# A two-layer hybrid transformer on one core: an out-projection put in program order, and two operations of the attention moved

## The chip, the cores and the metric

The kernel runs on one core of a Trainium2 chip. The metric is the device time of one execution in microseconds (us), given as the median of several runs. One further execution was taken by the hardware profiler; every row below comes from it, with times counted from the start of its span. The engines are TensorE (PE in the profile; its weight loads are PEld), VectorE (DVE), ScalarE (ACT), GpSimd (POOL) and SyncE (SP), which here issues most DMAs.

## The reference, cut to what matters

Layer 0 is grouped-query attention over 512 latent and 256 context tokens, followed by a gated FFN; layer 1 is a bidirectional Mamba-2 SSD mixer, followed by a gated FFN. The change touches the attention's inner loop and the SSD's last step.

```python
def gqa_attend(q, k, v):
    s = jnp.einsum('bqhgd,bkhd->bhgqk', q, k).astype(jnp.float32) * (HEAD_DIM ** -0.5)
    p = jax.nn.softmax(s, axis=-1).astype(v.dtype)
    return jnp.einsum('bhgqk,bkhd->bqhgd', p, v)
...
        y = yf + flip(yb) + d_skip[..., None] * xs
        y = rms_norm(y.reshape(bsz, length, D_INNER) * jax.nn.silu(z), norm_w) @ w_out
```

The out-projection takes 2048 gated values per token (D_INNER) to 1024 (D_MODEL); RMSNorm stands ahead of it. The model has 16 query heads of 64 and 4 key-value heads.

## The kernel before

Activations lie transposed, features on the 128 partitions and tokens along the free axis (L = 512 latent, C = 256 context, T = 768 together). A product of a weight tile and an activation tile is made of three matmuls, so that its precision is near float32: both operands are split into a high part (wh, and for activations names such as yh, hhy, qh) and a low part (wl, yl, hly, ql). `split` (L82 to L88) makes them: ScalarE casts the high part (L85), VectorE or GpSimd subtracts it from the original for the low part (L87). `load_w` loads a weight tile of 128 x 1024 (wst) and splits it; wst, wh and wl share one rotation of 10 buffers. `mm3` (L103) then issues wh times the high part (L108), wh times the low part (L109) and wl times the high part (L111).

The program is written as Python generators that are advanced by turns, and a scheduler then sets each engine's order from data dependencies and the order of the program; so an instruction can stand elsewhere than it is written. `behind(g, a, b)` adds a dependency of order alone: a comes after b on its engine.

**Attention.** The 16 heads are worked in 8 pairs p. `Pair.maxima` computes the scores once for their row maxima (ps_m, L643; VectorE's reduction ma and mb, L645) and puts the negated maxima on a diagonal (diag, L666). `Pair.steps` computes for each of 7 steps the scores of a key block for both heads (ps_s, L715) and adds the diagonal (L717); ScalarE takes the exponential of 128 x 1024 (pr, L718); VectorE adds it to a running sum (acc, L723 and L725); TensorE multiplies by the values (ps_o, L679). At a pair's end the sums come from a matmul (ps_sum, L685), ScalarE makes their reciprocal by logarithm and exponential (y, L688 and L689), and VectorE scales and corrects the output (o and u, L690 to L692). The scores have two PSUM buffers, shared by ps_s and ps_m: a score group waits for the exponential or the reduction that empties its buffer. The list `exps` holds the exponentials issued so far. Queries of later pairs are prepared beside this: `queries(p)` normalises and rotates the queries of pair p and splits them (qs to qh and ql, 128 x 768). For p from 4 to 7 the queries are also projected late: `qproj(p)` loads a weight tile, splits it with GpSimd making the low part, and projects (ps_q). The first of these, p = 4, is cast at a place in the values loop ahead of the pairs (`i == 30`).

**SSD's out-projection.** It stands at the end of `ssd` (L1290 on). Its 16 activation tiles are the gated products z times a norm weight, split by `ysplit` (ScalarE L1300, VectorE L1301) into hhy0 to hhy7 with their low parts hly, and, for the last eight, yh and yl. Their squares (ysq, L1231) are summed by GpSimd, and their row sums by TensorE (ssy, L247) give the norm's factor rsy, applied to the output. The loop over kp = 0 to 7 loads one weight tile each (wout0), covers two activation tiles k and four output tiles (`pm`, in ps_wo_13890 and ps_wo_13891): 2 x 4 x 3 = 24 matmuls. At kp == 4 output tile m = 4 is begun: `wm(4)` loads two weight tiles more (their high parts are wh_14141 and wh_14147), and `m_tile` runs its k = 0 to 7, again 24 matmuls, with hhy0 to hhy7 into ps_wo_14152. Its k = 8 to 15 follow behind the row sums, then the tiles m = 5 to 7. The weights of kp == 4 are wh_14135 and wl_14136.

Of the kernel before, what the change touches and what calls it, by code (L numbers as in the profile page):

```python
# [7 lines left out]
P = 128  # L8
# [7 lines left out]
D = 1024  # L16
KT = D // P
L = 512
# [62 lines left out]
def split(g, src, hi, lo, lo_engine="dve", pin=False):  # L81

    nc = g.nc
    keep = g.tc.keep_in_program_order if pin else lambda i: i
    cast = keep(nc.scalar.copy(hi, src))  # L85
    eng = nc.vector if lo_engine == "dve" else nc.gpsimd
    keep(eng.tensor_tensor(lo, src, _r(hi), ALU.subtract))  # L87
    return cast  # L88
# [14 lines left out]
def mm3(g, w, outs, first, last):  # L103

    wh, wl = w
    mm = g.nc.tensor.matmul
    for out, (ah, al) in outs:
        mm(out, wh, ah, start=first, stop=False)  # L108
        mm(out, wh, al, start=False, stop=False)  # L109
    for out, (ah, al) in outs:  # L110
        mm(out, wl, ah, start=False, stop=last)  # L111


def ada(g, src, layer, chunks, m0, nm, big=True):
# [111 lines left out]
def behind(g, bi, other):  # L226
    g.tc.add_manual_dep(bi.ins, other.ins.name, mybir.DependencyInfo(
        mybir.DependencyClass.NoSync, mybir.DependencyReason.DATA), reason="kept behind")
# [3 lines left out]
    follow(g, g.nc.scalar.preload_act_table_set("natural_log_exp_and_others"))  # L232


def rstd_rows(g, sq, n, cols, width, name, bank):

    nc = g.nc
    c = cols.shape[-1]  # L240
    nt = n // P
    ps = bank(f"ss{name}")
    w = nt * c
    sq = sq if isinstance(sq, list) else [sq]
    for i, part in enumerate(sq):
        for t in range(nt):
            nc.tensor.matmul(ps[:, i * w + t * c : i * w + (t + 1) * c], part[:, t * P : (t + 1) * P], cols,  # L247
                             start=True, stop=True)
    small = lambda nm: g.p.tile([P, nt * c], F32, tag="rst", bufs=8, name=nm)
    a, y, u = small("rsa"), small("rsy"), small("rsu")  # L250
    nc.vector.tensor_scalar(a, ps[:, :w], 1.0 / width, EPS, ALU.mult, ALU.add)
    if len(sq) == 2:
        nc.vector.scalar_tensor_tensor(a, ps[:, w : 2 * w], 1.0 / width, a, ALU.mult, ALU.add)

    for f in ((lambda: nc.scalar.activation(y, a, AF.Ln)), (lambda: nc.scalar.activation(y, y, AF.Exp, scale=-0.5))):
        g.root = f()
        if g.tables:
            follow(g, g.root)
    nc.vector.tensor_tensor(u, y, a, ALU.mult)
    nc.vector.scalar_tensor_tensor(u, y, -0.5, u, ALU.mult, ALU.mult)  # L260
    if c == 1:
        nc.vector.scalar_tensor_tensor(a, u, 1.5, y, ALU.add, ALU.mult)
        root = lambda t: a[:, t : t + 1].broadcast_to([P, P])
    else:
        rb = t3(g, f"rb{name}", n=n)
        wide = lambda v: v.unsqueeze(2).broadcast_to([P, nt * c, P // c])
        nc.vector.scalar_tensor_tensor(rb.rearrange("p (a b) -> p a b", b=P // c), wide(u), 1.5, wide(y),
                                       ALU.add, ALU.mult)
        root = lambda t: rb[:, t * P : (t + 1) * P]
    yield BREAK  # L270
    for t0 in range(0, nt, 4):
        pt = bank(f"rsT{name}")
        for t in range(t0, min(nt, t0 + 4)):
            nc.tensor.transpose(pt[:, (t - t0) * P : (t - t0 + 1) * P], root(t), g.ident)
        yield (pt, t0 * P, min(n, (t0 + 4) * P))
# [52 lines left out]
def Bank(g, name):  # L328
    return g.ps.tile([P, 512], F32, tag="B", bufs=4, name=name)
# [71 lines left out]
def attention(g, fill, X, late):  # L401


    nc, I = g.nc, g.I
# [61 lines left out]
    for m in range(KT):  # L466
        sq = t2("sql") if m else sums[0]
# [5 lines left out]
    norm = rstd_rows(g, sums, L, g.ones[:, :1], D, "a", Bk)  # L473
# [25 lines left out]
    for m in range(KT):  # L499
# [5 lines left out]
        if m in (1, 2):  # L505
            for a in range(4 * m - 4, 4 * m):
                sq = t2("sqc")[:, :C] if a else sqc
# [3 lines left out]
        if m == 3:  # L511
            norm = rstd_rows(g, sqc, C, g.ones[:, :1], D, "a", Bk)
# [73 lines left out]
    qprep = {}  # L586
# [3 lines left out]
    exps = []  # L590

    def qproj(p):

        st = t4(g, "wst")
        nc.sync.dma_start(st, I["wq"][p - 4])
        yield
        w = t4(g, "wh", F32R), t4(g, "wl", F32R)
        cast = split(g, st, *w, lo_engine="pool")
        if exps:
            behind(g, cast, exps[-1])  # L600
        yield
        qs = t3(g, "qs")
        for h, c0, n in ((hc, L, C), (hl, 0, L)):
            ps = Bk("ps_q")
            for k in range(KT):
                ks = slice(k * P, (k + 1) * P)
                mm3(g, (w[0][:, ks], w[1][:, ks]), [(ps[:, :n], h[k])], k == 0, k == KT - 1)
                yield 3 * n / 2400
            nc.scalar.copy(qs[:, c0 : c0 + n], ps[:, :n])
        qraw[p] = qs  # L610

    def queries(p, eng):
        qs = qraw[p]
        yield from normed(qs, g.qn8, eng)
        qprep[p] = t3(g, "qh", F32R), t3(g, "ql", F32R)
        split(g, qs, *qprep[p])
        yield 0

    onesr = g.const.tile([P, P], F32R, name="onesr")
# [116 lines left out]
    for n, j in enumerate((0, 1, 2, 4, 5, 3)):  # L736
        ps = Bk("ps_c")
# [73 lines left out]
    m = pairs[0].maxima()  # L811
    for i, _ in enumerate(vals):
        if i % 5 == 2:
            next(m, None)
        if i % 6 == 5:
            next(qgen[1], None)
        if i in (12, 26, 30, 34):
            next(qgen[2], None)
        if i == 16:
            next(side)  # L820
        if i == 30:
            next(items[1])
    for gen in (m, qgen[1], qgen[2]):
        for _ in gen:
# [2 lines left out]
    for p in range(NH // 2):  # L827
        m = iter(())
        if p < 7:
            m = pairs[p + 1].maxima()  # L830
# [165 lines left out]
def ssd(g, x, norm, wf, bg, close):  # L996


    nc, I, tc = g.nc, g.I, g.tc
# [4 lines left out]
    pool = lambda n, **k: ph.enter_context(tc.tile_pool(name=n, bufs=1, **k))  # L1004
# [20 lines left out]
    ps = ps_dt  # L1025
# [27 lines left out]
    for i in range(0, P, H2):  # L1053
        f, b = slice(i, i + 32), slice(i + 32, i + 64)
# [59 lines left out]
    acc = [None]  # L1114
# [125 lines left out]
    for gi in range(8):  # L1240
        i = -1
# [52 lines left out]
    ys = []  # L1294
# [17 lines left out]

    po = [S(g, "ps_wo") for _ in range(2)]
    pm = [po[i // 2][:, (i % 2) * 512 : (i % 2) * 512 + L] for i in range(4)]
    def m_tile(m, ws, ps, a, b, ks, bg=iter(())):
        for k in ks:
            c0 = (k % 8) * P
            mm3(g, tuple(w[:, c0 : c0 + P] for w in ws[k // 8]), [(ps, tuple(t[:, a:b] for t in ys[k]))],
                k == 0, k == 15)
            if k % 2:  # L1320
                next(bg, None)

    wm = lambda m: [load_w(g, I["wout1"][m - 4, i]) for i in range(2)]
    for kp in range(8):
        w = load_w(g, I["wout0"][kp])
        if kp == 4:
            ws, ps = wm(4), Bank(g, "ps_wo")
            m_tile(4, ws, ps, 0, L, range(2 * 4))
        for kk in range(2):
            ysplit()  # L1330
            k = 2 * kp + kk
            for i in range(4):
                c0 = kk * 512 + i * P
                mm3(g, (w[0][:, c0 : c0 + P], w[1][:, c0 : c0 + P]), [(pm[i], ys[k])], k == 0, k == 15)
        next(prev, None)
    ln_exp(g)
    norm = rstd_rows(g, acc[0], L, g.ones[:, :1], 2 * D, "y", lambda nm: Bank(g, nm))
    next(norm)
    m_tile(4, ws, ps, 0, L, range(2 * 4, 16))
    nc.scalar.copy(rs, next(norm)[0])  # L1340
# [6 lines left out]
    for m in (4, 5):  # L1347
        if m > 4:
            ws, ps = wm(m), Bank(g, "ps_wo")
# [7 lines left out]
    for seg in SEGS[0]:  # L1357
        _, a, b = seg
# [199 lines left out]
```

## Time and profile before

| What | us |
|---|---|
| runs of the kernel | 1860.58, 1860.64, 1859.17 |
| their median | 1860.58 |
| the profiled execution | 1859.79 |
| its span in the profile | 1858.0 |

In rows of the timeline the columns are the start, the duration, the engine, the line, the operation, output <- inputs, the shapes, and the count of merged instructions; brackets hold the idle time of the engine just before and what ended it. Times are in us from the span's start. Matmul rows of one group overlap, since a matmul starts before the one ahead of it has drained.

### The profile page before, as it was taken

What the parts mean: (1) busy time and instruction counts of PE and PEld (TensorE: products, weight loads), DVE (VectorE), ACT (ScalarE), POOL (GpSimd) and SP (SyncE); (2) the same over time, 40 slices, a digit from 0 to 9 for tenths busy, and PEclk for the clock granted to TensorE, in tenths of its full rate; (3) what the DMA queues carried; (4) which work ended last, traced back from release to release, by engine and by line L of the source; (5) the groups of instructions that cost most, each with busy time, mean ns of one, the idle gap of its engine ahead of it and who ended that gap; (6) DMA issues with size and microseconds to landing.
All of it is one profiled execution on the core that took longest, in us unless ns stands there. A gap on an engine that the chain in (4) does not pass through costs nothing.

```text
span 1858.0 us, 28773 instructions
## 1 busy us (share of the span) xinstructions
PE 1837.9 (99%) x11454; PEld 1540.3 (83%) x11454; DVE 1302.8 (70%) x1978; ACT 809.9 (44%) x1424; POOL 286.6 (15%) x260
## 2 busy tenths in 40 slices
PE   9999999999999999999999999999999999999999
PEld 7975656798888888888998888888887888888887
DVE  5578888788777776455487787777797566565655
ACT  4544434363222222222367666776666352323231
POOL 0223110030000000000133333444433100000000
PEclk9999999999999999999999999999999999999999
DMA  9323241124434553121224433444362223232232
GB/s 348 91 96 111 63 170 52 58 92 170 141 131 153 188 182 113 57 68 50 65 83 140 136 109 88 123 125 124 103 181 92 79 91 114 91 100 95 90 105 89
DMA packets 74071, 211.68 MB, mean 114 GB/s; under 512 B 9040, under 2 KB 14544, under 8 KB 73808
## 3 DMA queue, kind: packets, MB, share of 16 engines
q1 hardware_dynamic: 73936, 209.84, 35.0%
q8 instruction: 90, 1.47, 0.3%
q14 instruction: 45, 0.37, 0.1%
HBM read 198.79 MB, written 6.82 MB: 111 GB/s over the span
## 4 chain that ended last, share of the span: by engine, by line
PE 87%; DVE 6%; DMA 3%; issue 2%; ACT 1%; POOL 1%; SPq 0%; DVEq 0%; POOLq 0%; ACTq 0%
PE ps_up L108 10%; PE ps_up L111 10%; PE ps_up L109 10%; PE ps_d L108 7%; PE ps_d L109 6%; PE ps_d L111 6%; PE ps_in L111 5%; PE ps_in L109 5%; PE ps_in L108 4%; PE ps_s L715 2%; PE ps_o L679 2%; PE ps_st L1150 2%; PE ps_wo L109 1%; PE ps_wo L108 1%; PE ps_wo L111 1%
## 5 line engine op out<-in xcount | busy, mean ns | idle before, releaser
L87 DVE TENSOR_TENSOR wl<-wst,wh 128x1024 fp32r<-128x1024 f32 x207 | 258.5, 1249 | 202.8 <-PE ps_up L109 105.3
L85 ACT CAST wh<-wst 128x1024 fp32r<-128x1024 f32 x211 | 221.0, 1048 | 333.8 <-DMA wst<-in_wup 263.4
L108 PE MATMUL ps_up<-hhf,wh 128*128 128x512 f32 x1008 | 355.9, 353 | 0.0
L109 PE MATMUL ps_up<-hlf,wh 128*128 128x512 f32 x1008 | 355.8, 353 | 0.0
L111 PE MATMUL ps_up<-hhf,wl 128*128 128x512 f32 x1008 | 355.8, 353 | 0.0
L111 PEld LDWEIGHTS ps_up<-hhf,wl 128*128 128x128 f32 x1008 | 190.7, 189 | 25.9
L108 PEld LDWEIGHTS ps_up<-hhf,wh 128*128 128x128 f32 x1008 | 189.2, 188 | 25.9
L109 PEld LDWEIGHTS ps_up<-hlf,wh 128*128 128x128 f32 x1008 | 189.2, 188 | 25.9
L108 PE MATMUL ps_in<-hhs,wh 128*128 128x512 f32 (+1 forms) x560 | 203.7, 364 | 1.0 <-ACT dt L1035 1.0
L109 PE MATMUL ps_in<-hls,wh 128*128 128x512 f32 (+1 forms) x560 | 198.6, 355 | 0.0
L111 PE MATMUL ps_in<-hhs,wl 128*128 128x512 f32 (+1 forms) x560 | 198.3, 354 | 0.0
L108 PE MATMUL ps_d<-hdh,wh 128*128 128x512 f32 (+1 forms) x568 | 193.2, 342 | 0.8 <-DVE X L892 0.5
L109 PE MATMUL ps_d<-hdl,wh 128*128 128x512 f32 (+1 forms) x568 | 193.4, 341 | 0.0
L111 PE MATMUL ps_d<-hdh,wl 128*128 128x512 f32 (+1 forms) x568 | 192.8, 340 | 0.0
L892 DVE SCALAR_TENSOR_TENSOR X<-ps_d,mod,X 128x512 f32<-128x512 f32 (+1 forms) x224 | 125.2, 587 | 35.0 <-PE ps_d L111 34.3
L108 PEld LDWEIGHTS ps_in<-hhs,wh 128*128 128x128 f32 x560 | 105.5, 188 | 16.0 <-ACT dt L1035 1.2
L108 PEld LDWEIGHTS ps_d<-hdh,wh 128*128 128x128 f32 x568 | 106.5, 188 | 14.0 <-DVE X L892 0.9
L109 PEld LDWEIGHTS ps_d<-hdl,wh 128*128 128x128 f32 x568 | 106.9, 188 | 13.2 <-DVE hdl L87 0.4
L111 PEld LDWEIGHTS ps_d<-hdh,wl 128*128 128x128 f32 x568 | 107.6, 189 | 12.2
L111 PEld LDWEIGHTS ps_in<-hhs,wl 128*128 128x128 f32 x560 | 105.2, 188 | 14.8
L109 PEld LDWEIGHTS ps_in<-hls,wh 128*128 128x128 f32 x560 | 105.4, 188 | 13.4
L718 ACT ACTIVATE pr<-ps_s 128x1024 f32<-128x1024 f32 x56 | 57.2, 1022 | 105.1 <-PE ps_s L717 105.1
(343 smaller groups left out, 3629.8 us busy)
## 6 DMA issues: line engine op xcount, KB each, us to landing
wst<-in_wup SPq DMA_DIRECT2D x88, 512.0 KB, 3.4
wada<-in_adaT SPq DMA_DIRECT2D x56, 512.0 KB, 3.5
wst<-in_win SPq DMA_DIRECT2D x48, 512.0 KB, 3.6
wst<-in_wdown SPq DMA_DIRECT2D x44, 512.0 KB, 3.7
E<-ad SPq DMA_DIRECT2D x64, 256.0 KB, 6.6
wada<-in_adaB SPq DMA_DIRECT2D x24, 512.0 KB, 4.2
ec<-ead SPq DMA_DIRECT2D x64, 128.0 KB, 6.4
wst<-in_wout SPq DMA_DIRECT2D x16, 512.0 KB, 3.4
```

The lines of the kernel that those rows point to most:

```text
L85: cast = keep(nc.scalar.copy(hi, src))
L87: keep(eng.tensor_tensor(lo, src, _r(hi), ALU.subtract))
L108: mm(out, wh, ah, start=first, stop=False)
L109: mm(out, wh, al, start=False, stop=False)
L111: mm(out, wl, ah, start=False, stop=last)
L679: nc.tensor.matmul(po[S64[e], :n], v, pr[:, 512 * e + off : 512 * e + off + n], start=first, stop=last)
L715: nc.tensor.matmul(outs[e], kk[e][a][S64[e], k], b[S64[e], q], start=i == 0, stop=False)
L718: exps.append(nc.scalar.activation(pr, ps, AF.Exp))
L892: nc.vector.scalar_tensor_tensor(ap, o[:, c0:c1], gate[:, m, v : v + 1], ap, ALU.mult, ALU.add)
L1150: nc.tensor.matmul(ps[:, d * 256 : (d + 1) * 256], Bt[:, t * P : (t + 1) * P], xw[d][t], start=t == ts[0], stop=t == ts[-1])
```

## The change

There are three edits. First, `mm3` returns its matmuls, and in the out-projection `in_line` puts each group of three behind the group written before it; this covers the kp loop and output tile 4. The row sums are put behind the last group of the kp loop. Second, for p = 7 the cast of the queries is put behind the last exponential issued when it is written. Third, the low part of the first late query weights is made by VectorE, not GpSimd, and its place in the values loop moves from `i == 30` to `i == 36`.

```diff
     for out, (ah, al) in outs:
-        mm(out, wh, ah, start=first, stop=False)
-        mm(out, wh, al, start=False, stop=False)
+        seq.append(mm(out, wh, ah, start=first, stop=False))
+        seq.append(mm(out, wh, al, start=False, stop=False))
     for out, (ah, al) in outs:
-        mm(out, wl, ah, start=False, stop=last)
+        seq.append(mm(out, wl, ah, start=False, stop=last))
+    return seq
...
-            nc.tensor.matmul(ps[:, i * w + t * c : i * w + (t + 1) * c], part[:, t * P : (t + 1) * P], cols,
-                             start=True, stop=True)
+            mm = nc.tensor.matmul(ps[:, i * w + t * c : i * w + (t + 1) * c], part[:, t * P : (t + 1) * P], cols,
+                                  start=True, stop=True)
+            if after:
+                behind(g, mm, after)
...
-        cast = split(g, st, *w, lo_engine="pool")
+        cast = split(g, st, *w, lo_engine="pool" if exps else "dve")
...
-        split(g, qs, *qprep[p])
+        cast = split(g, qs, *qprep[p])
+        if p == 7:
+            behind(g, cast, exps[-1])
...
-        if i == 30:
+        if i == 36:
             next(items[1])
...
+    line = []
+
+    def in_line(seq):
+        if line:
+            behind(g, seq[0], line[-1])
+        line[:] = seq[-1:]
+
     def m_tile(m, ws, ps, a, b, ks, bg=iter(())):
         for k in ks:
             c0 = (k % 8) * P
-            mm3(g, tuple(w[:, c0 : c0 + P] for w in ws[k // 8]), [(ps, tuple(t[:, a:b] for t in ys[k]))],
+            seq = mm3(g, tuple(w[:, c0 : c0 + P] for w in ws[k // 8]), [(ps, tuple(t[:, a:b] for t in ys[k]))],
                 k == 0, k == 15)
+            if m == 4:
+                in_line(seq)
...
-                mm3(g, (w[0][:, c0 : c0 + P], w[1][:, c0 : c0 + P]), [(pm[i], ys[k])], k == 0, k == 15)
+                in_line(mm3(g, (w[0][:, c0 : c0 + P], w[1][:, c0 : c0 + P]), [(pm[i], ys[k])], k == 0, k == 15))
         next(prev, None)
     ln_exp(g)
-    norm = rstd_rows(g, acc[0], L, g.ones[:, :1], 2 * D, "y", lambda nm: Bank(g, nm))
+    norm = rstd_rows(g, acc[0], L, g.ones[:, :1], 2 * D, "y", lambda nm: Bank(g, nm), after=line[-1])
```

Line numbers of the changed kernel are higher: L108, L109 and L111 become L109, L110 and L112; L718 becomes L724, L688 L694, L1231 L1237, and L1300 L1306. Numbers behind a name tell its buffers apart.

ScalarE in the attention's last pairs but one, before: qh_3176 is the cast of the queries of p = 7, pr the exponentials, y the first step of a pair's end.

```order
L718 ACTIVATE pr_3076<-ps_s_3075 128x1024
L718 ACTIVATE pr_3137<-ps_s_3136 128x1024
L85 CAST qh_3176<-qs_2544 128x768
L718 ACTIVATE pr_3159<-ps_s_3158 128x1024
L718 ACTIVATE pr_3183<-ps_s_3182 128x1024
L688 ACTIVATE y_3221<-ps_sum_3218 128x512
```

And now:

```order
L724 ACTIVATE pr_3076<-ps_s_3075 128x1024
L724 ACTIVATE pr_3137<-ps_s_3136 128x1024
L724 ACTIVATE pr_3159<-ps_s_3158 128x1024
L85 CAST qh_3176<-qs_2544 128x768
L724 ACTIVATE pr_3183<-ps_s_3182 128x1024
L694 ACTIVATE y_3221<-ps_sum_3218 128x512
```

The cast stands one exponential later; VectorE's and TensorE's order there is the same as before.

TensorE in the out-projection, from the last group of kp == 3 (weights wh_14097) on, before:

```order
L108 MATMUL ps_wo_13891<-hhy7_14118,wh_14097 128x512
L109 MATMUL ps_wo_13891<-hly7_14119,wh_14097 128x512
L111 MATMUL ps_wo_13891<-hhy7_14118,wl_14098 128x512
L108 MATMUL ps_wo_13890<-yh_14177,wh_14135 128x512
L109 MATMUL ps_wo_13890<-yl_14178,wh_14135 128x512
L111 MATMUL ps_wo_13890<-yh_14177,wl_14136 128x512
...
L109 MATMUL ps_wo_13891<-yl_14178,wh_14135 128x512
L108 MATMUL ps_wo_14152<-hhy0_13898,wh_14141 128x512
L109 MATMUL ps_wo_14152<-hly0_13899,wh_14141 128x512
L111 MATMUL ps_wo_13891<-yh_14177,wl_14136 128x512
```

And now:

```order
L109 MATMUL ps_wo_13891<-hhy7_14118,wh_14097 128x512
L110 MATMUL ps_wo_13891<-hly7_14119,wh_14097 128x512
L112 MATMUL ps_wo_13891<-hhy7_14118,wl_14098 128x512
L109 MATMUL ps_wo_14152<-hhy0_13898,wh_14141 128x512
L110 MATMUL ps_wo_14152<-hly0_13899,wh_14141 128x512
L112 MATMUL ps_wo_14152<-hhy0_13898,wl_14142 128x512
L109 MATMUL ps_wo_14152<-hhy1_13914,wh_14141 128x512
...
L112 MATMUL ps_wo_14152<-hhy7_14118,wl_14142 128x512
L109 MATMUL ps_wo_13890<-yh_14177,wh_14135 128x512
```

The 24 matmuls of output tile 4 (ps_wo_14152), which stood among those of kp == 4 from its twelfth matmul on, now all stand ahead of them.

ScalarE at the same place, now; before, the same rows stand in the same order (with L1231 and L1300 for L1237 and L1306).

```order
L85 CAST wh_14135<-wst_14134 128x1024
L1237 ACTIVATE ysq_14093<-z_13741 128x512
L1306 ACTIVATE yh_14177<-z_12088,par_75 128x512
L1306 ACTIVATE yh_14193<-z_12136,par_75 128x512
L1306 ACTIVATE yh_14215<-z_12623,par_75 128x512
L1306 ACTIVATE yh_14231<-z_12671,par_75 128x512
L85 CAST wh_14141<-wst_14140 128x1024
L1306 ACTIVATE yh_14253<-z_13158,par_75 128x512
```

Nothing moved here: the cast of output tile 4's first weights stands behind four of the yh, and VectorE's low parts follow in the same order. Further on, the casts of later weights now stand ahead of the two steps on the norm's factor. On VectorE the low part of the first late query weights (wl_1433) now stands directly behind the diagonal of pair 0 and ahead of the next reduction; GpSimd has one subtraction fewer. SyncE's order is the same throughout.

More of the change, by code (lines that the diff above doesn't have):

```diff
@@ L106, in mm3 @@
     mm = g.nc.tensor.matmul
+    seq = []
     for out, (ah, al) in outs:
-        mm(out, wh, ah, start=first, stop=False)
-        mm(out, wh, al, start=False, stop=False)
+        seq.append(mm(out, wh, ah, start=first, stop=False))
+        seq.append(mm(out, wh, al, start=False, stop=False))
     for out, (ah, al) in outs:
-        mm(out, wl, ah, start=False, stop=last)
+        seq.append(mm(out, wl, ah, start=False, stop=last))
+    return seq
 def ada(g, src, layer, chunks, m0, nm, big=True):
@@ L232, in ln_exp, with rstd_rows @@
     follow(g, g.nc.scalar.preload_act_table_set("natural_log_exp_and_others"))
-def rstd_rows(g, sq, n, cols, width, name, bank):
+def rstd_rows(g, sq, n, cols, width, name, bank, after=None):
     nc = g.nc
```

## The prediction, made before the changed kernel was run

> **What bounds the kernel now.** First the page: TensorE is busy for 99% of the span, so only what makes it wait, or run at a lower clock, can move the end. Then the list of TensorE's waits over the whole span, for the places that the change touches.
>
> ```profile
> span 1858.0 us, 28773 instructions
> PE 1837.9 (99%) x11454; PEld 1540.3 (83%) x11454; DVE 1302.8 (70%) x1978; ACT 809.9 (44%) x1424; POOL 286.6 (15%) x260
> ```
>
> ```profile
> PE ps_s L715 <- ACT pr L718: 2.2, 2, 1.7
> PE ps_wo L109 <- DVE yl L1301: 1.0, 1, 1.0
> PE ps_m L643 <- DVE ma L645: 0.7, 1, 0.7
> PE ps_wo L108 <- ACT yh L1300: 0.5, 1, 0.5
> ```
>
> Columns: total us, number of waits, longest. The first wait is near the end of the attention (the cast moved by the second edit), the second and fourth lie in the SSD's out-projection (first edit). Together they are 1.7 + 1.0 + 0.5 = 3.2 us: no more than that can be won at the places named, and 0.2% of the time, about what a measurement of this kernel can tell from no change, is 3.7 us.
>
> Next the timeline of the attention stretch (start, duration, engine; in brackets the idle time before it and its releaser).
>
> ```profile
> 269.64 0.40 PE L717 MATMUL ps_s<-diag,onesr 64*128 64x512 f32 x2
> 271.13 1.22 DVE L645 TENSOR_REDUCE ma<-ps_m 128x2 f32<-128x1024 f32 x1
> 271.25 0.83 ACT L85 CAST qh<-qs 128x768 fp32r<-128x768 f32 x1 [2.81 <-DVE qs L570]
> 271.99 1.02 ACT L718 ACTIVATE pr<-ps_s 128x1024 f32<-128x1024 f32 x1
> 273.04 1.23 DVE L725 TENSOR_TENSOR acc<-acc,pr 128x1024 f32<-128x1024 f32 x1 [0.69 <-ACT pr L718]
> 273.06 0.38 PE L715 MATMUL ps_s<-qh,kh 64*128 64x256 f32 x1 [1.74 <-ACT pr L718]
> ...
> 274.18 0.95 DVE L87 TENSOR_TENSOR ql<-qs,qh 128x768 fp32r<-128x768 f32 x1
> ...
> 277.50 1.03 DVE L666 TENSOR_TENSOR diag<-id,mz 128x384 fp32r<-128x384 f32 x2
> 278.10 0.60 ACT L688 ACTIVATE y<-ps_sum 128x512 f32<-128x512 f32 x1 [2.69 <-PE ps_sum L685]
> 279.39 0.69 DVE L690 TENSOR_TENSOR o<-ps_o,y 128x512 f32<-128x512 f32 x1 [0.86 <-ACT y L689]
> 280.67 0.40 PE L717 MATMUL ps_s<-diag,onesr 64*128 64x512 f32 x2
> 287.20 1.22 DVE L645 TENSOR_REDUCE ma<-ps_m 128x2 f32<-128x1024 f32 x1
> 288.47 0.50 PE L643 MATMUL ps_m<-khs,qh 64*128 64x512 f32 x1 [0.69 <-DVE ma L645]
> ```
>
> The scores of the exponential at 271.99 were complete at 269.64 + 0.40 = 270.04, but the cast of the last queries stood ahead of it on ScalarE and itself waited for the queries until 271.25. So TensorE stood for 1.74 us. The windows of the same stretch (length, busy time of PE, PEld, DVE, ACT and POOL, granted TensorE clock, DMA share, GB/s) show two things more.
>
> ```profile
> 271.15:274.56 3.41, 1.67 (x24) 1.37 (x24) 2.72 (x4) 1.94 (x3) 0.00 (x0) 1.00 0.02 7
> 274.56:277.97 3.41, 3.41 (x8) 0.60 (x8) 3.32 (x8) 0.84 (x1) 0.00 (x0) 0.50 0.00 0
> 279.39:288.42 9.03, 7.92 (x69) 4.03 (x60) 8.96 (x17) 7.28 (x12) 0.00 (x0) 1.00 0.04 16
> 960.64:964.05 3.41, 2.41 (x21) 2.21 (x21) 1.00 (x3) 3.35 (x8) 0.00 (x0) 1.00 0.46 159
> 964.05:967.46 3.41, 3.41 (x22) 3.01 (x21) 3.38 (x3) 2.77 (x3) 0.00 (x0) 1.00 0.00 0
> ```
>
> After 3.41 us of which TensorE was busy for 1.67, its granted clock was 0.50 for the next 3.41 us. A stretch of the same length with 2.41 busy was followed by 1.00. And from 279.39 to 288.42 VectorE is busy for 8.96 of 9.03 us: it sets the pace there, TensorE only waits for it at the end (0.69 us at 288.47).
>
> **Part by part: the cast behind the exponential.** The exponential can start at about 270.1 and end at 271.1; the cast, whose queries are there at 271.25, keeps its own time. TensorE's 1.74 us go, and with them the stretch at half clock. What is late next is VectorE. Its order is unchanged, so its queue can move up only by its own idle time: 0.69 us ahead of the accumulation at 273.04 and 0.86 us ahead of the product at 279.39 (with the sums done earlier, ScalarE's two steps on them end before VectorE gets there), and some 0.1 at each of the two joints, where back-to-back instructions overlap by that much (273.04 + 1.23 = 274.27 lies 0.1 past the next start, 274.18). That is 0.69 + 0.86 + 0.15 = 1.7 us. Behind 279.39 it has 0.07 us of idle left. TensorE runs further ahead at first: today the diagonal is ready at 277.50 + 1.03 = 278.53 and its scores come at 280.67 only because TensorE is late; now the diagonal itself, some 0.75 earlier, sets them at about 277.8, 2.86 us earlier. But the reduction that TensorE waits for at 288.47 comes only 1.7 earlier, so of 2.86 some 1.1 is given back, and the wait grows from 0.69 to about 1.8 us. Net **-1.7** (bounds -1.3, if one joint gives nothing, and -1.8, all that VectorE has).
>
> That wait is as long as the 1.74 that went. Whether the clock falls again depends on how much of the idle time one stretch of 3.41 us holds: 3.41 - 1.8 = 1.6 busy is as little as the 1.67 after which it fell, but a boundary through the wait leaves both sides above 2.4, after which it did not. The three times shown, 1859.17 to 1860.64, differ by 1.5 us, about one half-clock stretch (3.41 / 2 = 1.7). So it costs 0 to 1.7, in about half the positions; I take **+0.85**.
>
> **The first late query weights.** VectorE takes over the low part.
>
> ```profile
> 103.52 1.03 DVE L666 TENSOR_TENSOR diag<-id,mz 128x384 fp32r<-128x384 f32 x2
> 107.65 1.23 DVE L645 TENSOR_REDUCE ma<-ps_m 128x4 f32<-128x1024 f32 x1 [3.10 <-PE ps_m L643]
> ```
>
> ```profile
> 104.85 2.39 POOL L87 TENSOR_TENSOR wl<-wst,wh 128x1024 fp32r<-128x1024 f32 x1 [7.65 <-PE ps_v L551]
> 113.56 0.28 PE L111 MATMUL ps_q<-hha,wl 128*128 128x256 f32 x1
> ```
>
> The buffer that the low part is written to came free at about 104.8, when GpSimd began. On VectorE it takes 1.21 us (the row at 1424.11 below, same shape), so it ends at about 106.1, inside the 3.10 us in which VectorE stands idle until 107.65. TensorE reads it at 113.56. GpSimd is rid of 2.39 us, with its rotary products behind it starting earlier. **0**; without that cover it would be 1.2, since the reduction behind it is waited for.
>
> **The out-projection in program order.** Now the rows around its last gated pair.
>
> ```profile
> 1419.42 0.63 ACT L1231 ACTIVATE ysq<-z 128x512 f32<-128x512 f32 x1 [5.24 <-DVE z L1229]
> 1419.86 0.39 PE L111 MATMUL ps_wo<-hhy,wl 128*128 128x512 f32 x1
> 1419.96 2.54 ACT L1300 ACTIVATE yh<-z,par 128x512 fp32r<-128x512 f32 x4
> 1420.71 0.49 PE L108 MATMUL ps_wo<-yh,wh 128*128 128x512 f32 x1 [0.47 <-ACT yh L1300]
> 1422.26 0.50 PE L109 MATMUL ps_wo<-yl,wh 128*128 128x512 f32 x1 [1.05 <-DVE yl L1301]
> 1422.41 1.03 ACT L85 CAST wh<-wst 128x1024 fp32r<-128x1024 f32 x1
> 1422.59 0.40 PE L111 MATMUL ps_wo<-yh,wl 128*128 128x512 f32 x1
> 1422.83 0.39 PE L108 MATMUL ps_wo<-yh,wh 128*128 128x512 f32 x1
> 1424.11 1.21 DVE L87 TENSOR_TENSOR wl<-wst,wh 128x1024 fp32r<-128x1024 f32 x1
> 1424.65 0.39 PE L108 MATMUL ps_wo<-hhy,wh 128*128 128x512 f32 x1
> ```
>
> From 1422.83 to 1424.65 there are 8 starts, so a matmul takes 1.82 / 8 = 0.2275 us. Today TensorE goes on with the yh matmuls, whose weights are long there. In the new order the 24 matmuls of output tile 4 stand ahead of them, and their weights are those cast at 1422.41. ScalarE's order up to that cast and VectorE's up to the low part are the same as before (behind the square that waits for z until 1419.42, and four yh), so neither can come earlier. The first matmul waits for the cast's end, 1422.41 + 1.03 = 1423.44, and starts at about 1423.5: TensorE idles from 1419.86 + 0.39 = 1420.25 for 3.25 us, where it now waits 0.47. The second follows. The third needs the low part, 1424.11 + 1.21 = 1425.32, and starts at 1425.4, after about 1.1 us of waiting. The fourth starts 0.33 later (as 1422.26 to 1422.59) at 1425.72; today's fourth started at 1422.83. So **+2.9**: 3.25 + 1.1 of new waits, less the 0.47 + 1.05 that go, and the rest in the third pair's overlap. The joints are good to 0.2 either way. Behind it nothing is late:
>
> ```profile
> 1434.57 1.03 ACT L85 CAST wh<-wst 128x1024 fp32r<-128x1024 f32 x1
> 1430.00:1440.00 10.00, 10.00 (x50) 8.32 (x49) 4.10 (x7) 2.40 (x4) 0.00 (x0) 1.00 0.49 159
> ```
>
> The third cast, today at 1434.57, then waits for tile 4's first half, whose last matmul ends at about 1425.7 + 21 x 0.2275 = 1430.5; with 1.03 and 1.21 it is complete at 1432.8. Its readers come two groups of 24 later, 1430.5 + 48 x 0.2275 = 1441.4. TensorE is already busy for the whole of 1430 to 1440 and can absorb no delay, so the 2.9 reach the end. The row sums, now behind the eighth pair, and VectorE's and ScalarE's steps on them lie beside tile 4's second half, 24 x 0.2275 = 5.5 us.
>
> The clock comes on top. Between 1420.25 and 1425.4 TensorE would be busy for some 0.7 us. However 3.41 us stretches fall on that, one of them holds at most 1.7 us of work, and 1.67 was followed by 0.50. The half-clock stretch costs half of what it would have done: 1.7 where it begins with the fourth matmul, little where it lies mostly over the second wait. Laid over this timeline at all offsets it gives 0.3 to 2.1; I take **+1.2**.
>
> The Trainium skill ("TensorE: Matmul & The Clock Gate", Part 1, the table of the two states) says that the clock returns to half after at least one idle window of about 3.4 us. The trace differs: a stretch with 1.67 us of work was enough here. By that rule the 3.25 us of idle time might leave the clock up, and the sum would be 1.2 lower, or 2.05 with the attention's term.
>
> **Sum.** -1.7 + 0.85 + 0 + 2.9 + 1.2 = +3.25 on the profiled execution's 1859.79. The median of the runs, 1860.58, is 0.79 above that: **1863.8**.
>
> **The rivals.** (b) *The clock falls in the attention nearly every time as well.* The new wait for VectorE's reduction decides this, once it leaves less than some 2 us of work in a stretch. For it: it is as long as the wait that did this at 273.06. Against: that one lay whole in one stretch. Both clock terms near their upper part: -1.7 + 1.7 + 2.9 + 1.2 to 2.0 = +4.1 to +4.9, 1864.7 to 1865.5: slower than the 3.7 us of the bound.
> (c) *The clock does not fall in the out-projection*, since something other than the share of work in a stretch sets it. For it: 2.41 of 3.41 did not do it, so the border is seen from two points only. Against: the wait here leaves less work than the 1.67. Then -1.7 + 2.9, with 0 to 0.85 for the attention: +1.2 to +2.05, 1861.8 to 1862.6. With the clock left up in both and the attention at its best, 1861.0. The rule of the Trainium skill named above leads here; the trace's 0.50 after 1.67 speaks against it.
> (d) *The out-projection does what program order seems to promise*: tile 4's weights are there in time, TensorE works through them while yh and yl are made, and 0.47 + 1.05 go. For it: the matmuls moved up read values made long before. Against: their weights' cast stands behind the four yh on ScalarE, in both orders. It would give -1.7 - 1.5 = -3.2, 1857.4, with 0.5 more at best.
>
> **How the numbers follow.** The forecast case has 0.53, (b) 0.22, (c) 0.15, (d) 0.06; 0.04 remain for something of no shown size, counted as no change. The bound of "slower" is 1860.58 + 3.7 = 1864.3. The forecast case lies 0.5 below it and, with its clock terms at 0.3 to 2.1 and 0 to 1.7, passes it in about a fifth: 0.43 no change and 0.10 slower. (b) is slower, (c) no change, (d) lies at the lower bound, 1856.9, and is halved. Faster 0.03, the same 0.43 + 0.15 + 0.03 + 0.04 = 0.65, slower 0.10 + 0.22 = 0.32. The range runs from (c)'s lower end, 1861.0, to 0.3 past (b)'s upper, 1865.8; it leaves out (d), the remainder and some edges.
>
> **What would show it right or wrong.** Right: a wait of about 3.2 us ahead of the first hhy matmul of output tile 4, ended by ScalarE's cast, and one of 1.1 ahead of its third, ended by VectorE's low part; a granted clock of 0.50 in a stretch close behind; no wait at the exponential near 271, but one of about 1.8 us for the reduction near 286; nothing new near 105. Wrong: tile 4's cast ending before 1421, the attention's end (today 288.47) earlier by other than 1.7, or a wait of over 0.5 us for weights behind 1430.

## The result, and the profile after

The changed kernel takes 1863.62 us (median of 17 runs, 1862.77 to 1865.56); the kernel before, run beside it, 1860.12 (17 runs, 1858.27 to 1862.09). The ratio is 1.0021, with a 95% interval of 1.0014 to 1.0028: slower by 3.5 us by the medians, at the bound of what was called no change, and 0.2 from the forecast's 1863.8. The profiled execution took 1863.02 us, its span 1861.2, 3.2 more than the 1858.0 of before.

TensorE's list of waits after the change, the rows at the places of the change (us in total, times, longest):

```profile
PE ps_wo L109 <- ACT wh L85: 3.3, 1, 3.3
PE ps_m L649 <- DVE ma L651: 1.6, 1, 1.6
PE ps_wo L112 <- DVE wl L87: 1.1, 1, 1.1
```

The waits for yh, yl and the exponential are gone. In their place stand one for the cast of tile 4's weights, one for their low part, and a longer one for VectorE's reduction. The timeline of the out-projection shows the first two at work.

```profile
1418.19 0.63 ACT L1237 ACTIVATE ysq<-z 128x512 f32<-128x512 f32 x1 [5.25 <-DVE z L1235]
1418.73 2.54 ACT L1306 ACTIVATE yh<-z,par 128x512 fp32r<-128x512 f32 x4
1421.18 1.03 ACT L85 CAST wh<-wst 128x1024 fp32r<-128x1024 f32 x1
1422.26 0.50 PE L109 MATMUL ps_wo<-hhy,wh 128*128 128x512 f32 x1 [3.26 <-ACT wh L85]
1422.88 1.21 DVE L87 TENSOR_TENSOR wl<-wst,wh 128x1024 fp32r<-128x1024 f32 x1
1424.14 0.72 PE L112 MATMUL ps_wo<-hhy,wl 128*128 128x512 f32 x1 [1.15 <-DVE wl L87]
1424.65 0.63 PE L109 MATMUL ps_wo<-hhy,wh 128*128 128x512 f32 x1
```

The cast ends at 1421.18 + 1.03 = 1422.21 and the matmul starts at 1422.26. From 1424.14 on a matmul takes 0.72 and 0.63 us, not 0.39: the clock is down. The windows (columns as in the prediction) say for how long; the fourth and fifth lie around the reduction's wait in the attention, the last two near the start of the kernel.

```profile
1417.43:1420.84 3.41, 1.57 (x7) 0.95 (x6) 3.20 (x4) 2.65 (x5) 1.45 (x1) 1.00 0.28 70
1420.84:1424.25 3.41, 0.84 (x3) 0.41 (x4) 3.41 (x6) 3.41 (x6) 0.00 (x0) 1.00 0.22 87
1424.25:1427.66 3.41, 3.41 (x9) 2.64 (x10) 3.41 (x5) 2.30 (x3) 0.00 (x0) 0.50 0.03 5
284.20:287.61 3.41, 1.82 (x8) 0.38 (x4) 3.41 (x5) 2.63 (x4) 0.00 (x0) 1.00 0.23 88
287.61:291.02 3.41, 3.41 (x17) 1.25 (x15) 3.41 (x5) 0.73 (x1) 0.00 (x0) 1.00 0.90 268
11.14:14.55 3.41, 2.94 (x80) 2.70 (x80) 2.12 (x11) 0.73 (x5) 0.00 (x0) 1.00 1.04 407
14.55:17.96 3.41, 3.25 (x15) 3.17 (x15) 1.87 (x6) 1.88 (x3) 2.29 (x3) 0.50 1.04 397
```

One half-clock stretch follows the out-projection's waits, none the attention's, and one lies near the start, where the execution of before has none.

The mean granted clock of every execution is on record too. A half-clock stretch takes 3.41 x 0.5 / 1858 = 0.0009 off it, so 1.000 is an execution without such a stretch, 0.999 one with one, 0.998 one with two. The changed kernel has 0.998 in 12 of its 17 executions, 0.997 in one and 0.996 in four; these four are its slowest, 1865.25 to 1865.56.

The attention's rows:

```profile
270.14 0.40 PE L723 MATMUL ps_s<-diag,onesr 64*128 64x512 f32 x2
270.58 1.02 ACT L724 ACTIVATE pr<-ps_s 128x1024 f32<-128x1024 f32 x1 [1.64 <-PE ps_s L723]
271.81 0.38 PE L721 MATMUL ps_s<-qh,kh 64*128 64x256 f32 x1
278.23 0.68 DVE L696 TENSOR_TENSOR o<-ps_o,y 128x512 f32<-128x512 f32 x1
278.37 0.50 PE L723 MATMUL ps_s<-diag,onesr 64*128 64x512 f32 x2 [0.24 <-DVE diag L672]
285.92 1.21 DVE L651 TENSOR_REDUCE ma<-ps_m 128x2 f32<-128x1024 f32 x1
287.18 0.50 PE L649 MATMUL ps_m<-khs,qh 64*128 64x512 f32 x1 [1.59 <-DVE ma L651]
```

The exponential starts as its scores end, VectorE has no idle time ahead of its product at 278.23, and the gain ends in the wait at 287.18. And the third edit:

```profile
105.25 1.23 DVE L87 TENSOR_TENSOR wl<-wst,wh 128x1024 fp32r<-128x1024 f32 x1 [0.21 <-PE ps_v L555]
108.15 1.22 DVE L651 TENSOR_REDUCE ma<-ps_m 128x4 f32<-128x1024 f32 x1 [1.67 <-PE ps_m L649]
```

The low part took a place in which VectorE had nothing to do; 1.67 us of that idle time are left.

To see where the time went, each matmul's start was compared with that of the same matmul in the trace of before, and the medians of these shifts were taken over short stretches. The shift goes from +0.5 behind the kernel's start to -1.3 behind the attention (288 to 297 us), stays between -1.2 and -1.6 as far as 1416, and goes from -1.25 to +3.21 over the out-projection: -1.8 in the one, +4.5 in the other, and nothing at 105, where it is 0.5 on both sides. The +0.5 of the start is no effect of the change: the traces of the experiments have 0.0 to 0.7 there.

### The profile page after: what moved, and what is told of

Same layout as the page of the kernel before. It is cut to its first block, busy times and chain, and to the rows that moved or that the text cites. A ratio compares the mean times of both kernels' runs of the same rounds, so it can differ in the third digit from the quotient of the medians.

```text
span 1861.2 us, 28778 instructions
## 1 busy us (share of the span) xinstructions
PE 1839.3 (99%) x11454; PEld 1542.0 (83%) x11454; DVE 1305.2 (70%) x1979; ACT 810.3 (44%) x1424; POOL 286.9 (15%) x259
## 4 chain that ended last, share of the span: by engine, by line
PE 86%; DVE 7%; DMA 3%; issue 2%; ACT 1%; POOL 0%; SPq 0%; DVEq 0%; POOLq 0%; ACTq 0%
PE ps_up L109 10%; PE ps_up L110 10%; PE ps_up L112 10%; PE ps_d L109 7%; PE ps_d L110 6%; PE ps_d L112 6%; PE ps_in L112 5%; PE ps_in L110 5%; PE ps_in L109 4%; PE ps_s L721 2%; PE ps_o L685 2%; PE ps_st L1156 2%; PE ps_wo L109 1%; PE ps_wo L112 1%; PE ps_wo L110 1%
## 5 line engine op out<-in xcount | busy, mean ns | idle before, releaser
L109 PE MATMUL ps_up<-hhf,wh 128*128 128x512 f32 x1008 | 355.9, 353 | 0.0
L110 PE MATMUL ps_up<-hlf,wh 128*128 128x512 f32 x1008 | 355.8, 353 | 0.0
L112 PE MATMUL ps_up<-hhf,wl 128*128 128x512 f32 x1008 | 355.8, 353 | 0.0
L112 PEld LDWEIGHTS ps_up<-hhf,wl 128*128 128x128 f32 x1008 | 190.6, 189 | 25.8
L109 PEld LDWEIGHTS ps_up<-hhf,wh 128*128 128x128 f32 x1008 | 189.2, 188 | 26.0
L110 PEld LDWEIGHTS ps_up<-hlf,wh 128*128 128x128 f32 x1008 | 189.2, 188 | 25.9
L109 PE MATMUL ps_in<-hhs,wh 128*128 128x512 f32 (+1 forms) x560 | 203.7, 364 | 1.0 <-ACT dt L1041 1.0
L110 PE MATMUL ps_in<-hls,wh 128*128 128x512 f32 (+1 forms) x560 | 198.6, 355 | 0.0
L112 PE MATMUL ps_in<-hhs,wl 128*128 128x512 f32 (+1 forms) x560 | 198.3, 354 | 0.0
L109 PE MATMUL ps_d<-hdh,wh 128*128 128x512 f32 (+1 forms) x568 | 193.2, 342 | 0.8 <-DVE X L898 0.5
L110 PE MATMUL ps_d<-hdl,wh 128*128 128x512 f32 (+1 forms) x568 | 193.3, 341 | 0.0
L112 PE MATMUL ps_d<-hdh,wl 128*128 128x512 f32 (+1 forms) x568 | 192.8, 340 | 0.0
L109 PEld LDWEIGHTS ps_in<-hhs,wh 128*128 128x128 f32 x560 | 105.5, 188 | 16.0 <-ACT dt L1041 1.2
L109 PEld LDWEIGHTS ps_d<-hdh,wh 128*128 128x128 f32 x568 | 106.4, 188 | 14.0 <-DVE X L898 0.9
L110 PEld LDWEIGHTS ps_d<-hdl,wh 128*128 128x128 f32 x568 | 106.9, 188 | 13.2 <-DVE hdl L87 0.4
L112 PEld LDWEIGHTS ps_d<-hdh,wl 128*128 128x128 f32 x568 | 107.6, 189 | 12.2
L112 PEld LDWEIGHTS ps_in<-hhs,wl 128*128 128x128 f32 x560 | 105.2, 188 | 14.8
L110 PEld LDWEIGHTS ps_in<-hls,wh 128*128 128x128 f32 x560 | 105.4, 188 | 13.4
L724 ACT ACTIVATE pr<-ps_s 128x1024 f32<-128x1024 f32 x56 | 57.2, 1022 | 106.5 <-PE ps_s L723 106.5
```

Source lines behind the costliest of these rows:

```text
L109: seq.append(mm(out, wh, ah, start=first, stop=False))
L110: seq.append(mm(out, wh, al, start=False, stop=False))
L112: seq.append(mm(out, wl, ah, start=False, stop=last))
L724: exps.append(nc.scalar.activation(pr, ps, AF.Exp))
```

## The experiments

**The out-projection's order alone.** The changed kernel without its other two edits.

```diff
-        cast = split(g, st, *w, lo_engine="pool" if exps else "dve")
+        cast = split(g, st, *w, lo_engine="pool")
...
-        if p == 7:
-            behind(g, cast, exps[-1])
...
-        if i == 36:
+        if i == 30:
```

> The out-projection's order alone (first edit), without the other two. The changed kernel's trace shows 2.9 us of waits for tile 4's weights and 1.5 us of half clock behind them. If the edits add up, this kernel is slower than the kernel before by 4.4 us (2.9 if the half clock was a chance of one execution). If part of the loss came from the attention's earlier end colliding with something later, it is slower by clearly less than 4.4, or by 2.9 with a clock that stays up.

Measured: 1863.76 us against 1859.45, ratio 1.0020 (1.0011 to 1.0029), 4.3 us slower. The loss needs neither of the other edits. In its trace two half-clock stretches follow the waits:

```profile
1422.40:1425.80 3.40, 2.63 (x6) 1.63 (x7) 3.40 (x5) 3.40 (x6) 0.00 (x0) 0.51 0.03 7
1425.80:1429.20 3.40, 3.40 (x10) 2.62 (x9) 3.26 (x4) 0.81 (x1) 0.00 (x0) 0.50 0.12 18
```

So the shift over the out-projection is 5.25 here (-1.20 to +4.05), against 4.46 in the changed kernel's trace. And it showed something of the kernel before that the first trace could not: the attention is as before here, with the same 1.7 us wait for the exponential, but this time the clock did not fall behind it, and the shift over the attention is -1.0 (0.63 to -0.39). The half clock at 274.56 in the trace of before had thus cost 1.0 us. VectorE's product, which had 0.86 us of idle time ahead of it there, has none here:

```profile
279.13 0.68 DVE L694 TENSOR_TENSOR o<-ps_o,y 128x512 f32<-128x512 f32 x1
```

**The attention's edits alone.** The changed kernel without `in_line`'s dependencies and without that of the row sums.

```diff
-        if line:
-            behind(g, seq[0], line[-1])
...
-    norm = rstd_rows(g, acc[0], L, g.ones[:, :1], 2 * D, "y", lambda nm: Bank(g, nm), after=line[-1])
+    norm = rstd_rows(g, acc[0], L, g.ones[:, :1], 2 * D, "y", lambda nm: Bank(g, nm))
```

> The second and third edit alone; the out-projection's order is left to the scheduler as before. By the theory that the attention's gain is real and carried to the end: faster than before by 1.5 to 1.8 us, up to 1.7 less in executions where the clock falls behind the new wait for VectorE's reduction. By the rival that the gain is given back before the end: no difference over 0.5 us.

Measured: 1858.31 against 1859.45, ratio 0.9994 (0.9986 to 1.0003): 1.1 us faster, not separated from zero by the runs. The trace's shift is -1.8 over the attention (0.53 to -1.29) and +0.1 over the out-projection, and the -1.3 reached behind the attention is still -1.1 at 1300. So next to nothing is given back; but it is -1.8 against an execution with a half clock there, and -0.8 against the one of the run above without it. The median lies between. In the executions with a granted clock of 1.000, few as they are, the medians are 1858.06 (7 of 11) and 1858.76 (11 of 33 of the kernel before): 0.7 apart, close to the 0.8. The trace's span is 2.6 us shorter than that of before; 1.5 of this was won between 1300 and 1404, where nothing was changed, and the trace of the filled kernel below won as much there. One trace's span is thus no measure of the change; the shift over a stretch is.

**Tile 4's weights loaded first.** The changed kernel with two loads exchanged. TensorE's order and the kinds and places of ScalarE's instructions stay; only the two casts change places: tile 4's now stands ahead of the square, that of kp == 4 behind four yh.

```diff
     for kp in range(8):
+        if kp == 4:
+            ws, ps = [load_w(g, I["wout1"][0, 0])], Bank(g, "ps_wo")
         w = load_w(g, I["wout0"][kp])
         if kp == 4:
-            ws, ps = wm(4), Bank(g, "ps_wo")
+            ws.append(load_w(g, I["wout1"][0, 1]))
```

> The changed kernel, with the first weight tile of output tile 4 loaded ahead of that of kp == 4, so that its cast takes the place ahead of the square on ScalarE; TensorE's order stays that of the changed kernel. If the loss came from where the cast stands on ScalarE: both waits for the weights go, so do the two for yh and yl that the kernel before had (0.47 and 1.05), tile 4's matmuls follow without a gap, and the time is about 2 us less than with the attention's edits alone, 3.5 to 4 us below the kernel before. If the loss came from holding TensorE to the written order as such: still slower than before by 1 us or more.

Measured: 1856.91 against 1859.45, ratio 0.9986 (0.9977 to 0.9995): 2.5 us faster. The timeline of its out-projection: tile 4's weights are cast at 1413.77, ahead of the square; its matmuls follow kp == 3 without a gap, and the cast at 1423.03 is now that of weights which are read after them.

```profile
1413.77 1.03 ACT L85 CAST wh<-wst 128x1024 fp32r<-128x1024 f32 x1
1420.04 0.63 ACT L1237 ACTIVATE ysq<-z 128x512 f32<-128x512 f32 x1 [5.24 <-DVE z L1235]
1420.71 0.39 PE L109 MATMUL ps_wo<-hhy,wh 128*128 128x512 f32 x1
1420.93 0.39 PE L110 MATMUL ps_wo<-hly,wh 128*128 128x512 f32 x1
1421.20 0.50 PE L112 MATMUL ps_wo<-hhy,wl 128*128 128x512 f32 x1
1423.03 1.04 ACT L85 CAST wh<-wst 128x1024 fp32r<-128x1024 f32 x1
```

The shift over the out-projection is -1.9 (0.62 to -1.32), where the changed kernel has +4.5: with the same order on TensorE, 6.4 us lie in which cast stands first. The written order as such costs nothing. The total missed its expectation (3.5 to 4 us). In the profiled execution, the slowest of the eleven, the clock fell behind the attention's new wait: the shift there is only -0.3 (0.45 to 0.19), and the window behind it reads

```profile
288.80:292.20 3.40, 3.40 (x13) 1.46 (x12) 3.40 (x5) 1.05 (x2) 0.00 (x0) 0.50 0.91 327
```

By the granted clock, 8 of the 11 executions hold at least one such stretch; where they lie, only the trace shows. The three at 1.000 have a median of 1855.96, 2.8 below the 1858.76 of the kernel before at 1.000, and 0.8 + 1.9 = 2.7. So the expectation was too high also because it took the attention's gain at the size that it has against an execution with a half clock.

**The wait filled with matmuls.** The changed kernel with 14 extra matmuls ahead of tile 4's first; they write to the same PSUM bank, which tile 4's first matmul then starts anew.

```diff
             ws, ps = wm(4), Bank(g, "ps_wo")
+            for _ in range(14):
+                in_line([nc.tensor.matmul(ps[:, :L], wprev[0][:, :P], ys[0][0], start=True, stop=True)])
...
+        wprev = w
```

> The changed kernel, with 14 matmuls added ahead of tile 4's first, whose results are overwritten; they take 14 x 0.2275 = 3.2 us, about all of the wait for the cast. The work of the kernel and both waits' ends stay. If the 1.5 us beyond the waits are the half clock: no stretch at 0.50 behind the wait, and the time is 1.2 to 1.5 us below that of the changed kernel, 1.4 to 2.0 above the kernel before. If they are something else: the same time as the changed kernel, or more.

Measured: 1861.34 against 1859.45, ratio 1.0008 (0.9999 to 1.0017): 1.9 us slower than the kernel before, where the changed kernel was 3.5 slower.

```profile
1416.91 3.33 PE L1344 MATMUL ps_wo<-hhy,wh 128*128 128x512 f32 x14
1420.37 0.50 PE L109 MATMUL ps_wo<-hhy,wh 128*128 128x512 f32 x1
1422.27 0.50 PE L112 MATMUL ps_wo<-hhy,wl 128*128 128x512 f32 x1 [1.17 <-DVE wl L87]
1422.61 0.40 PE L109 MATMUL ps_wo<-hhy,wh 128*128 128x512 f32 x1
```

Matmuls take 0.40 behind the wait, the granted clock is 1.00 all through, and the shift over the out-projection is +2.9 (-3.18 to -0.26). So the changed kernel's 4.46 is 2.9 of waiting and 1.5 of half clock. The granted clock is 1.000 in 8 of its 11 executions, and in none of the changed kernel's 17. Keeping TensorE busy with work that nobody reads made the changed kernel faster, by 1.6 us by the medians.

**Tile 4 behind the group of kp == 4.** The changed kernel with the first half of tile 4 written one group later.

```diff
             ws, ps = wm(4), Bank(g, "ps_wo")
-            m_tile(4, ws, ps, 0, L, range(2 * 4))
...
+        if kp == 4:
+            m_tile(4, ws, ps, 0, L, range(2 * 4))
         next(prev, None)
```

> The changed kernel with output tile 4's first half written, and so held, behind the group of kp == 4 instead of ahead of it; the weights' casts keep their places on ScalarE. If only the place of tile 4 against its weights' cast cost the time: no wait for that cast, the waits for yh and yl return (0.5 and 1.0 us, as in the kernel before), the out-projection takes what it took before, and the time is that of the attention's edits alone, 1 to 2 us below the kernel before. If holding TensorE to a written order costs by itself: slower than the attention's edits alone by over 1 us.

Measured: 1858.76 against 1858.95, ratio 0.9997 (0.9988 to 1.0006). Its waits in the out-projection are those of the kernel before:

```profile
PE ps_wo L110 <- DVE yl L1307: 1.0, 1, 1.0
PE ps_wo L109 <- ACT yh L1306: 0.5, 1, 0.5
```

The shift over the out-projection is 0.0 (-2.26 to -2.24) and over the attention -1.8. Its median is 0.2 below that of the kernel before, where the attention's edits alone were 1.1 below and 1 to 2 was expected; the two intervals overlap, so the runs do not tell these apart, and it is the trace that agrees with the theory.

**VectorE relieved, by GpSimd.** The kernel with the loads exchanged; in addition GpSimd makes one low part that VectorE made just ahead of the reduction.

```diff
-                wos.append(load_w(g, I["w_o"][t * P : (t + 1) * P], after=exps[-1]))
+                wos.append(load_w(g, I["w_o"][t * P : (t + 1) * P], after=exps[-1],
+                                  lo_engine="pool" if t == 0 else "dve"))
```

> The kernel with the two weight loads exchanged, with one operation more moved: the low part of the first weight tile of the attention's own out-projection is made by GpSimd (2.39 us, idle there), not by VectorE (1.22 us), in the stretch where the changed kernel waits 1.6 us for VectorE's reduction. If VectorE's queue sets that wait: it falls to 0.4 to 0.6, the stretch ends 1.0 to 1.2 us earlier, and the clock does not fall behind it; in all 4.5 to 5 us below the kernel before. If ScalarE's exponentials or TensorE's own scores set it: the wait stays at about 1.6 and the time at that of the kernel with the exchange alone.

Measured: 1857.59 against 1858.95, ratio 0.9991 (0.9982 to 1.0): no better than the exchange alone. The wait grew from 1.6 to 2.2 us; the first row is the copy with the exchange alone, the others are of this kernel:

```profile
282.17 0.16 DVE L655 COPY mb<-ma 128x4 f32<-128x4 f32 x1
...
282.01 2.79 POOL L87 TENSOR_TENSOR wl<-wst,wh 128x1024 fp32r<-128x1024 f32 x1 [13.93 <-ACT wh L85]
282.48 2.35 DVE L655 COPY mb<-ma 128x4 f32<-128x4 f32 x1
285.75 1.21 DVE L651 TENSOR_REDUCE ma<-ps_m 128x2 f32<-128x1024 f32 x1
287.01 0.49 PE L649 MATMUL ps_m<-khs,qh 64*128 64x512 f32 x1 [2.18 <-DVE ma L651]
```

A copy of 128x4 took 2.35 us on VectorE, where it takes 0.16 in the kernel with the loads exchanged. It ends at 284.83, GpSimd's operation at 284.80. VectorE was rid of 1.22 us ahead of the reduction, and a sum (1.21) and an output correction (0.41) also came to stand behind it; but VectorE was held for 2.2, and the reduction ends at 286.96, against 287.06 with the exchange alone. TensorE waits longer for it because it gets there earlier: two of its value matmuls (ps_o) now stand behind the wait. The attempt thus says little on whether VectorE sets the wait.

**The copy as a two-operand instruction.** As the last, with one line more.

```diff
-            nc.vector.tensor_copy(ctx[:, :, 4:], lat[:, :, 4:])
+            nc.vector.tensor_tensor(ctx[:, :, 4:], lat[:, :, 4:], lat[:, :, 4:], ALU.min)
```

> As the kernel before it (weight loads exchanged, one low part on GpSimd), with the copy of the context maxima (128x4, L655) written as a minimum of two equal operands on VectorE. There the copy had taken 2.35 us instead of 0.16 and ended with GpSimd's 2.79 us operation. If the copy was held by GpSimd's operation, and a two-operand instruction is not, as the subtraction of 0.68 us that ran beside it was not: the minimum takes 0.2 us, VectorE's reduction ends 2 us earlier against its neighbours, TensorE's wait for it falls from 2.2 to under 0.5 us, and the attention's stretch ends 1.1 to 1.6 us earlier than with the exchange alone, without a half clock behind it; 4.5 to 5 us below the kernel before. If any VectorE instruction at that place is held: 2 us again and no gain. If the wait is not VectorE's at all: 0.2 us for the minimum, and TensorE still waits about 1.6 us, for something else.

Measured: 1857.63 against 1859.38, ratio 0.9992 (0.9983 to 1.0001). The second expectation came true, not the first:

```profile
281.48 2.79 POOL L87 TENSOR_TENSOR wl<-wst,wh 128x1024 fp32r<-128x1024 f32 x1 [13.94 <-ACT wh L85]
281.95 2.34 DVE L655 TENSOR_TENSOR mb<-ma 128x4 f32<-128x4 f32 x1
```

It is held just the same, to 284.29 against GpSimd's 284.27. The subtraction that seemed to run beside GpSimd was there first, and GpSimd had 2.79 us instead of its 2.39, as if it had waited for that.

**VectorE relieved, by order.** The kernel with the loads exchanged, with the same low part left on VectorE, but put behind the reduction.

```diff
+                g.red = nc.vector.reduce_max(...)
...
+                if t == 0:
+                    st, wh, wl = t4(g, "wst"), t4(g, "wh", F32R), t4(g, "wl", F32R)
+                    nc.sync.dma_start(st, I["w_o"][:P])
+                    behind(g, nc.scalar.copy(wh, st), exps[-1])
+                    wos.append((wh, wl))
+                else:
+                    wos.append(load_w(g, I["w_o"][t * P : (t + 1) * P], after=exps[-1]))
+                if t == 1:
+                    behind(g, nc.vector.tensor_tensor(wl, st, _r(wh), ALU.subtract), g.red)
```

> The kernel with the two weight loads exchanged, with VectorE relieved without GpSimd: the same low part of 1.22 us is put behind the reduction that TensorE waits for (its cast stays; two other steps, a sum and an output correction, also come to stand behind that reduction, and the low part's first reader on TensorE comes later). If VectorE's queue sets the 1.6 us wait: the reduction ends 1.2 to 2.8 us earlier, the wait falls to under 0.5 us, the attention's stretch ends 1.1 to 1.6 us earlier than with the exchange alone in an execution without half clock, and no half clock follows; 4.5 to 5 us below the kernel before. If something else sets it, or the work put off is what is late next: TensorE still waits 1 us or more between the same two points, for the sum or the low part, and the time is that of the exchange alone.

Measured: 1855.33 against 1860.17, ratio 0.9974 (0.9964 to 0.9985): 4.8 us faster than the kernel before, and the fastest here. Its 8 runs lie between 1854.80 and 1855.97, six of them at a granted clock of 1.000 and none below 0.999; with the exchange alone 3 of 11 are at 1.000.

```profile
283.46 1.22 DVE L651 TENSOR_REDUCE ma<-ps_m 128x2 f32<-128x1024 f32 x1
284.73 0.50 PE L649 MATMUL ps_m<-khs,qh 64*128 64x512 f32 x1
```

Three operations of VectorE now stand behind the reduction instead of ahead of it: the low part (1.22 us) and the sum (1.21) and output correction (0.41) of the last attempts. The reduction ends at 284.68, 2.4 us earlier than in the changed kernel, and TensorE goes on without an idle stretch; here too two of its value matmuls come behind. In its list of waits for 266 to 310 us two small ones take the place of the 1.6:

```profile
PE ps_d L112 <- DVE wl L87: 0.4, 1, 0.4
PE ps_d L109 <- ACT wh L85: 0.4, 1, 0.4
```

The shift over the attention is -2.8 (0.67 to -2.12), 1.0 better than the attention's edits alone at full clock, and over the out-projection -1.9. VectorE's queue did set the wait. The span is 4.6 us shorter than that of before (1853.4 against 1858.0): -2.8 and -1.9, with +0.7 at the start and -0.6 between the two places, which other executions have otherwise.

## Why the prediction was right, point by point

**The out-projection's waits: right in mechanism and size.** Forecast were 3.25 and 1.1 us of waiting and 2.9 in all; the trace has 3.26 and 1.15, and the filled kernel, in which no half clock hides it, 2.9. The exchange of loads showed the cause: the cast's place on ScalarE, not the order on TensorE.

**Its clock term: right, and a little small.** The 1.2 was 1.5 in the changed kernel's trace and 5.25 - 2.9 = 2.3 with the order alone, the latter just past the forecast's upper end of 2.1. Rival (c), by which the clock stays up, did not come about. The stretch after which it fell in the changed kernel's trace had 0.84 us of work in it. By the Trainium skill's rule of at least one idle window of about 3.4 us ("TensorE: Matmul & The Clock Gate", Part 1) the 3.26 us of idle time might have left it up; the trace differs, and the measurement decides.

**The attention: right against the profiled execution, for a reason that was half told.** The -1.7 was -1.8, the new wait for the reduction 1.6 instead of 1.8, and TensorE's scores came at 278.37 - 0.5 = 277.9 where 277.8 was forecast. The step that was missing: the 0.86 us that VectorE idled ahead of 279.39 in the trace of before were the work of the half clock behind the old wait. In the run with the order alone, where the clock stayed up behind the same wait, VectorE does not idle there, and the stretch is 1.0 shorter. So against such an execution the edit is worth only 0.8. The prediction made its sum against one execution, and did not ask what the old wait costs in those where the clock stays up.

**The attention's clock: as uncertain as forecast.** The 0.85 stood for 1.7 in half the positions. Of the five traces with the wait of 1.6 us, it fell behind it in one (the exchange of loads; its shift is 1.5 short of the others'). The two with 2.2 us fell both. Of the 44 executions of the four experiments with the wait of 1.6 us, 22 have a granted clock of 1.000, so it fell nowhere in them. Rival (b), in which it falls nearly always, is not borne out. The changed kernel's four upper runs, to 1865.56 at a granted clock of 0.996, reach its time, but no trace shows where their further half-clock stretches lie.

**The third edit: nothing, as forecast.** It took 1.23 us of 3.10 idle.

**The sum.** In the two profiled executions it is +0.5 (at the start, not of the change) - 1.8 + 4.5 = 3.2, against a forecast of 3.25; the parts that were missed, 0.5 at the start, 0.85 in the attention, 0.35 in the out-projection, happen to cancel. By the medians it is 3.5. That the forecast came within 0.2 is thus in part luck; that the waits came where and as long as forecast is not. The lower end of the range, 1861.0, does not follow from its terms: with the clock up and the attention at its best, -1.8 + 2.9 on the median of 1860.58 is 1861.7. That rival (d) fell was clear from ScalarE's order; the exchange of loads makes it come true, at -1.9 where (d) had -1.5.

## What to carry to other kernels

Before putting matmuls in a wished order, look where the instruction that makes their operand stands on its own engine: that order decides, and exchanging two loads was worth 6.4 us in the traces, 6.0 by the medians, where the order on TensorE was the same. A wait of TensorE's can cost more than its length, since the clock may be halved behind it, and a trace of one execution holds such a stretch or not: compare stage by stage, and look at the granted clock of both traces. When a wait is removed, follow the next queue that was hidden behind it; here a subtraction put behind a reduction, with a sum and a correction that came along, gave a further 1.0 us.

## What the runs showed of the hardware

VectorE and GpSimd kept each other out: a 128x4 copy, and a 128x4 minimum as well, took 2.35 and 2.34 us on VectorE instead of 0.16 and ended within 0.03 us of GpSimd's subtraction, which itself took 2.79 us instead of 2.39 having started during a VectorE subtraction. The Trainium skill ("SBUF — State Buffer", Who interferes with whom) says that the two share a pair of ports under an exclusive lock, that a copy can need it and that a VectorE instruction with two inputs in SBUF contends with a GpSimd instruction that reads SBUF; the traces agree.

What makes the clock fall is not settled. After 1.67 us of busy time in a stretch of 3.41 us (before), 1.79 and 1.25 (the two attempts with GpSimd, below) and 0.84 (after) it fell. After 1.82 it fell in one trace (loads exchanged, ahead of 288.80) and not in another (after, 284.20), nor after 1.81 in a third (the order alone, 272.15). After 1.57 it did not (after, 1417.43), and near the start it did after 2.94 (after, 11.14).

```profile
285.39:288.80 3.41, 1.79 (x7) 0.57 (x7) 3.41 (x6) 1.68 (x3) 0.00 (x0) 1.00 0.21 78
283.17:286.58 3.41, 1.25 (x10) 0.71 (x10) 3.41 (x6) 3.37 (x6) 1.10 (x1) 1.00 0.00 0
```

So the busy time of the profile alone does not decide. The matmuls differ: at 1417.43 the weights are 128*128, in the attention 64*128 and 128*64, and near the start the outputs are 128x1 or the weights 128*32. That may be the difference; no run tried it.
